# A 3x3 convolution with max pooling: input rows cast to bf16 by the loads, fewer five-product steps, and a new order of work

## The chip, the cores and the metric

The kernel runs on one core of a Trainium2 chip. The metric is device time in microseconds of that core, the median of several runs. A core has a matrix engine (PE, with its weight loads shown as PEld), a vector engine (DVE), a scalar engine (ACT), a general engine (POOL, also called GpSimd) and a queue engine (SP) that only issues DMAs here. Matrix products are summed in PSUM (8 banks of 128 x 512 f32); everything else lies in SBUF.

## The reference

The input x is 16 images of 64 channels, 64 by 64, in f32. The weights are 128 x 64 x 3 x 3. The reference pads each image by one, convolves, and takes the maximum of each 2 by 2 block:

```
x_pad = np.pad(x, ((0, 0), (0, 0), (pad, pad), (pad, pad)), mode='constant')
conv[b, co] += weight[co, ci, kh, kw] * x_pad[b, ci, kh:kh+h, kw:kw+w]
output[b, c, i, j] = np.max(conv[b, c, i*2:(i+1)*2, j*2:(j+1)*2])
```

The output is 16 x 128 x 32 x 32 in f32.

## The kernel before, in words

*Pairs, quarters, steps.* Two images (a pair p, 0 to 7) lie in one SBUF tile: image 0's 64 channels on partitions 0 to 63, image 1's on 64 to 127. Each image is cut into four quarters q of 16 rows, which give R = 8 rows of pooled output. A pair and a quarter are a step s, 32 in all. In a product the image number l (0 or 1, called a lane) picks one half of the PE array's rows, so that a matmul of lane 0 and one of lane 1 can run side by side. A matmul's output is 128 channels by 8 rows by 64 columns, one PSUM bank.

*Two convolution rows for one pooled row.* A step makes, per lane, a sum A and a sum B in two banks, from which the even and the odd convolution rows follow. Each product takes three matmuls, one per horizontal tap kw (`taps`, L406 to L421). There are two recipes, chosen per step by SEQ:

- A W step takes four products. Their inputs are made from the input rows first: E (differences of two neighbouring rows), S (sums) and V (differences of rows two apart; Ve and Vo are its two halves). P2 (on E) and P0 (on V) go to A. A is then copied to B (`seed`, L435, written SE in the order, SEv when DVE does it), P3 and P1 are added to B, and A's negative is evacuated (`evac`, EV, L429).
- A K step takes five products, PAa, PAb, PBa, PBb straight on bf16 input rows and PR on KS (a sum of neighbouring rows). It needs no seed and only the KS row operation.

After that both go on alike: the row maximum of B and the evacuated A (`rowmax`, MX, L449, DVE), a copy of the odd columns to SBUF (`odd`, OD, L472, ACT), and the maximum of even and odd columns (`colmax`, CM, L481, DVE), then the store (ST).

*Where the rows come from.* W steps read f32 tiles `wx` (four of them, each for a whole pair, with a row of zeros above and below); SP loads them (LX). K steps read bf16 tiles `kx` (a pool of 3); the first two K steps and step 2 go by way of an f32 tile `kf` and casts on ACT or DVE (XO, XE), the rest by a DMA from POOL's queue that casts on its way (LK, L275). Eight steps are K, 24 are W.

*Who makes the rows.* A suffix in the order names the engine: E.8:v on DVE, V.8:g on POOL, :a on ACT. For eleven W steps ACT first copies a row to a PSUM bank (`lift`, CP, L290), and DVE reads that copy beside the SBUF row (`two_rows`, L294). A row operation on POOL is made to wait for the last row operation that stands before it on DVE (`row_op`, L195 to L200).

*What sets the order.* ORDER is one list written out by hand, or rather by a search; each engine runs its part of it in order, and semaphores join the engines. Products are emitted in groups (`flush`): two products of different lanes give their taps by turns. `paced` (L251) makes a load wait until the step 12 (W) or 13 (K) before it has done its column maximum, since the tiles are used again.

*Head.* The weights are loaded first (LW), seven blocks of them are formed (c.D0, c.GS, ... on DVE; c.g0, c.g1, c.g2 on ACT), turned by PE (T) and copied out to SBUF (TV).

Of the kernel before, what the change touches and what calls it, by code (L numbers as in the profile page):

```python
# [9 lines left out]

SEQ = "KWKWWKWWWKWWWWKWWWKWWWWKWWWKWWWW"
ADDED = ()
ORDER = """
LW c.GS:v c.D2:v c.GM:v c.g1:a T.G1:0 T.D2:1 LX.1 c.D0:v c.g2:a E.1:v c.g0:a T.GM:2 TV.G1:a c.GP:v
T.G0:3 Ve.1:v T.D0:4 LX.0a TV.GM:a TV.G0:a TV.D0:a P2.1.1:5 P2.1.0:6 TV.D2:a SE.1.0:7 XO.0a:v T.G2:0
TV.G2:v SE.1.1:2 T.GP:3 Vo.1:v LX.0b PAa.0.1a:4 PAa.0.0a:1 XE.0a:a P0.1.0 P0.1.1 XO.0b:v S.1:v
PBa.0.0a:0 PAb.0.1a LX.3 P3.1.1 P3.1.0 TV.GP:a XE.0b:a LX.2 LX.4 PBa.0.0b PBa.0.1a:3 LX.6 EV.1.0  # L20
LK.5 PAb.0.0a PAa.0.1b EV.1.1 PBb.0.0a PBb.0.1a Vo.3:v KS.0:v MX.1.0 CP.3:6 PBa.0.1b PAa.0.0b Ve.3:g
PAb.0.1b PBb.0.0b PAb.0.0b PBb.0.1b XO.2:a XE.2:a E.4:g MX.1.1 EV.0.1 E.3:v P1.1.0 PAa.2.1:5 EV.0.0
PAa.2.0:4 P1.1.1 S.3:v MX.0.1 OD.1.0 OD.1.1 S.4:g Ve.4:g CP.6:6 PBa.2.0:1 PAb.2.1 MX.0.0 CM.1.0 LX.8
LX.7 CM.1.1 EV.2.1 PAb.2.0 PR.0.1 PR.0.0 PBa.2.1:7 EV.2.0 OD.0.0 OD.0.1 P2.3.0:2 P2.3.1:5 E.6:v
S.6:v KS.2:v CM.0.1 P2.4.0:4 PBb.2.1 CM.0.0 LX.10 LX.11 SE.3.1:6 PBb.2.0 P0.3.1 SE.4.0:3 SE.3.0:0
P0.4.0 P3.3.1 MX.2.1 EV.3.1 Vo.4:g EV.4.0 V.6:v P0.3.0 PR.2.1 LK.9 EV.3.0 LK.14 MX.2.0 MX.3.1
P2.4.1:5 P3.3.0 MX.3.0 P2.6.1:4 PR.2.0 SE.4.1:2 LX.12 OD.2.1 CM.2.1 OD.2.0 P1.3.1 P3.4.0 CM.2.0
S.7:g MX.4.0 OD.3.1 P1.3.0 P0.4.1 SE.6.1:7 OD.3.0 V.7:g EV.4.1 P2.6.0:1 P3.4.1 P0.6.1 P1.4.0 CM.3.1
SE.6.0:6 CM.3.0 E.7:v P3.6.1 PAa.5.0:5 EV.6.1 OD.4.0 V.10:g E.10:g MX.4.1 CM.4.0 MX.6.1 CP.8:4
PAa.5.1:0 P0.6.0 E.8:v P1.4.1 PAb.5.0 S.8:v EV.6.0 P3.6.0 PAb.5.1 EV.5.0 P2.7.1:3 PBa.5.0:1 EV.5.1  # L30
OD.4.1 MX.6.0 P1.6.1 P2.7.0:5 SE.7.1:0 PBa.5.1:4 PBb.5.0 OD.6.1 CM.4.1 S.10:v SE.7.0:2 P1.6.0 P0.7.1
KS.5:v CM.6.1 MX.5.0 P0.7.0 PBb.5.1 EV.7.1 EV.7.0 V.8:g P3.7.0 P2.10.1:7 PR.5.0 P3.7.1 MX.5.1 MX.7.0
PAa.9.0:3 PR.5.1 SE.10.1:5 OD.6.0 KS.14:v CM.6.0 V.11:g LX.16 P0.10.1 P1.7.0 MX.7.1 OD.5.0 OD.5.1
CM.5.1 OD.7.0 P3.10.1 P2.8.0:6 EV.10.1 SE.8.0:4 LX.15 LX.13 P1.7.1 PAb.9.0 EV.9.0 CM.5.0 MX.10.1
PBa.9.0:7 P2.8.1:1 OD.7.1 CM.7.0 KS.9:v P1.10.1 P0.8.0 SE.8.1:3 OD.10.1 CM.7.1 PAa.14.1:2 PBb.9.0
EV.8.0 LK.18 S.12:v E.12:g CP.11:0 CM.10.1 P3.8.0 P0.8.1 V.12:g PAa.9.1:6 P2.10.0:5 EV.8.1 MX.9.0
MX.8.0 SE.10.0:1 E.11:v PR.9.0 PAb.14.1 OD.9.0 PAb.9.1 P1.8.0 E.15:g EV.14.1 OD.8.0 P3.8.1 P0.10.0
S.11:v P2.11.1:0 PAa.14.0:2 CM.9.0 CP.13:7 CM.8.0 PBa.9.1:4 P3.10.0 MX.8.1 E.13:v EV.10.0 EV.9.1
P1.8.1 PAb.14.0 P2.11.0:5 PBb.9.1 MX.10.0 S.13:v SE.11.1:6 EV.14.0 OD.8.1 P1.10.0 P0.11.1 MX.9.1
SE.11.0:2 ST.5 OD.10.0 P3.11.1 P2.12.0:7 EV.11.1 CM.8.1 SE.12.0:3 ST.1 LX.17 ST.3 MX.11.1 ST.0  # L40
CM.10.0 P0.11.0 PR.9.1 OD.9.1 EV.11.0 V.13:g P2.13.1:0 P3.11.0 P0.12.0 P1.11.1 SE.13.1:1 CM.9.1
V.15:g MX.11.0 KS.18:v OD.11.1 CM.11.1 P3.12.0 P2.12.1:5 EV.12.0 SE.12.1:4 E.16:g P1.11.0 P0.13.1
LX.19 OD.11.0 MX.12.0 P3.13.1 PBa.14.0:7 EV.13.1 LX.20 P2.13.0:6 P0.12.1 LX.22 CM.11.0 PBb.14.0
# [40 lines left out]
def kernel(  # L84
# [7 lines left out]
    nc = tc.nc  # L92
# [13 lines left out]
    assert len(SEQ) == N  # L106

    const = ctx.enter_context(tc.tile_pool(name="const", bufs=1))
    kx_pool = ctx.enter_context(tc.tile_pool(name="kx_pool", bufs=3))
    row_pool = ctx.enter_context(tc.tile_pool(name="row_pool", bufs=8))  # L110
    v_pool = ctx.enter_context(tc.tile_pool(name="v_pool", bufs=6))
    vh_pool = ctx.enter_context(tc.tile_pool(name="vh_pool", bufs=4))
    ev_pool = ctx.enter_context(tc.tile_pool(name="ev_pool", bufs=8))
    od_pool = ctx.enter_context(tc.tile_pool(name="od_pool", bufs=6))
    od2_pool = ctx.enter_context(tc.tile_pool(name="od2_pool", bufs=4))
# [142 lines left out]
    def load(s, part, e):  # L258
# [11 lines left out]
        if e == "a":  # L270
            behind(inst, begun)
# [342 lines left out]
```

## Time and profile before

| what | value |
|---|---|
| median of 3 runs | 103.51 us (103.31 to 103.87) |
| span of the profiled execution, first to last instruction | 101.5 us |
| PE busy | 96.4 us, 870 matmuls |
| DVE busy | 91.4 us, 181 instructions |
| ACT busy | 89.5 us, 198 instructions |
| POOL busy | 79.3 us, 65 instructions |
| DMA | 24.07 MB, mean 237 GB/s |

The profiled execution has a span of 101.5 us; what lies around it is in the runs' times, whose median is 2.0 us more. Times in the profile count from the start of the span. In a row of a group stand the line, the engine, the operation, output and inputs, shape and count; then busy time in us, the mean of one in ns, and the idle time before it with what ended it. In a row of the timeline stand start and duration in us.

### The profile page before, as it was taken

What the parts mean: (1) busy time and instruction counts of PE and PEld (TensorE: products, weight loads), DVE (VectorE), ACT (ScalarE), POOL (GpSimd) and SP (SyncE); (2) the same over time, 40 slices, a digit from 0 to 9 for tenths busy, and PEclk for the clock granted to TensorE, in tenths of its full rate; (3) what the DMA queues carried; (4) which work ended last, traced back from release to release, by engine and by line L of the source; (5) the groups of instructions that cost most, each with busy time, mean ns of one, the idle gap of its engine ahead of it and who ended that gap; (6) DMA issues with size and microseconds to landing.
All of it is one profiled execution on the core that took longest, in us unless ns stands there. A gap on an engine that the chain in (4) does not pass through costs nothing.

```text
span 101.5 us, 2486 instructions
## 1 busy us (share of the span) xinstructions
PE 96.4 (95%) x870; PEld 55.6 (55%) x870; DVE 91.4 (90%) x181; ACT 89.5 (88%) x198; POOL 79.3 (78%) x65
## 2 busy tenths in 40 slices
PE   6999999999999999999989999999999999999950
PEld 2356885466666666555645555455475555655510
DVE  0599999999999999799999989998999999888980
ACT  5599999999988999998999989989989889899840
POOL 7000898988598599989999999998599999999000
PEclk9999999999999999999999999999999999999999
DMA  2999999991079989889998999999953915302353
GB/s 45 328 248 403 417 376 337 326 226 33 6 203 390 233 166 302 315 222 291 273 329 260 261 237 311 374 392 308 295 222 122 344 58 201 108 29 78 110 189 121
DMA packets 13789, 24.07 MB, mean 237 GB/s; under 512 B 1104, under 2 KB 9680, under 8 KB 13776
## 3 DMA queue, kind: packets, MB, share of 16 engines
q1 hardware_dynamic: 12624, 22.16, 64.9%
q0 software_dynamic: 864, 1.56, 10.2%
q10 hardware_dynamic: 288, 0.20, 0.6%
q8 instruction: 7, 0.11, 0.4%
q14 instruction: 6, 0.05, 0.1%
HBM read 17.07 MB, written 8.39 MB: 251 GB/s over the span
## 4 chain that ended last, share of the span: by engine, by line
PE 83%; ACT 6%; DVE 3%; DMA 3%; issue 2%; DVEq 0%; ACTq 0%
PE acc L414 80%; DMA wraw<-in_weight_dram 3%; ACT acc L445 3%; PE acc L229 2%; DVE acc L449 2%; ACT od L472 2%; ACT ev L429 1%; DVE o L481 1%; ACT wq L191 1%; DVE acc L443 0%; PE acc L439 0%; DVEq L609 0%; DVEq L449 0%; DVEq L443 0%; ACTq L290 0%
## 5 line engine op out<-in xcount | busy, mean ns | idle before, releaser
L414 PEld LDWEIGHTS <-wt 64*128 64x128 bf16 x840 | 52.8, 94 | 37.3 <-issue 2.5
L414 PE MATMUL acc<-wv,wt 64*128 64x504 bf16 (+1 forms) x228 | 49.5, 377 | 0.3 <-ACT acc L445 0.3
L449 DVE TENSOR_TENSOR acc<-acc,ev 128x512 f32<-128x512 f32 x64 | 42.9, 693 | 2.0 <-ACT ev L429 1.1
L196 POOL TENSOR_TENSOR wv<-wx 128x1024 bf16<-128x1024 f32 x18 | 42.3, 2362 | 2.5 <-DVE ks L196 1.6
L414 PE MATMUL acc<-kx,wt 64*128 64x504 bf16 (+6 forms) x216 | 38.9, 350 | 0.0
L414 PE MATMUL acc<-ws,wt 64*128 64x512 bf16 (+1 forms) x144 | 35.2, 377 | 0.2 <-DVE acc L449 0.2
L414 PE MATMUL acc<-we,wt 64*128 64x512 bf16 (+1 forms) x144 | 35.1, 377 | 0.0
L429 ACT ACTIVATE ev<-acc 128x512 f32<-128x512 f32 x48 | 28.6, 610 | 1.1 <-PE acc L414 1.0
L445 ACT COPY acc<-acc 128x512 f32<-128x512 f32 x45 | 26.3, 588 | 2.0 <-PE acc L414 0.4
L481 DVE TENSOR_TENSOR o<-acc,od 128x256 f32<-128x256 f32 (+1 forms) x65 | 25.7, 412 | 1.4 <-ACT od L472 0.5
L472 ACT COPY od<-acc 128x256 f32<-128x256 f32 x64 | 23.6, 382 | 2.7 <-PE acc L414 1.9
L196 POOL TENSOR_TENSOR we<-wx 128x512 bf16<-128x512 f32 x11 | 14.0, 1272 | 2.8 <-DVE ks L196 1.7
L414 PE MATMUL acc<-ks,wt 64*128 64x504 bf16 (+1 forms) x48 | 12.5, 377 | 0.0
L414 PE MATMUL acc<-vh,wt 64*128 64x504 bf16 (+1 forms) x60 | 10.4, 376 | 0.0
L196 POOL TENSOR_TENSOR ws<-wx 128x512 bf16<-128x512 f32 x8 | 10.1, 1268 | 0.1
L275 POOL DMA_DIRECT2D kx<-in_x_dram x6 | 3.5, 590 | 8.0 <-ACT ev L429 8.0
L431 ACT COPY ev<-acc 128x512 f32<-128x512 f32 x16 | 9.3, 598 | 0.4 <-PE acc L414 0.3
L196 POOL TENSOR_TENSOR vh<-wx 128x512 bf16<-128x512 f32 x7 | 8.8, 1272 | 0.5 <-DVE ks L196 0.4
L294 DVE TENSOR_TENSOR we<-acc,wx 128x512 bf16<-128x512 f32 x11 | 7.5, 682 | 0.0
L294 DVE TENSOR_TENSOR ws<-acc,wx 128x512 bf16<-128x512 f32 x11 | 7.5, 681 | 0.0
L290 ACT COPY acc<-wx 128x512 f32<-128x512 f32 x11 | 6.7, 607 | 0.1
L509 PE MATMUL acc<-const-bfloat16-1.0 128*128 128x512 bf16 x8 | 3.6, 625 | 0.8 <-PEq L595 0.8
(30 smaller groups left out, 34.3 us busy)
## 6 DMA issues: line engine op xcount, KB each, us to landing
out_dram<-o SPq DMA_DIRECT2D x30, 256.0 KB, 5.8
wx<-in_x_dram SPq DMA_DIRECT2D x12, 512.0 KB, 6.3
wx<-in_x_dram SPq DMA_DIRECT2D x6, 544.0 KB, 6.5
wx<-in_x_dram SPq DMA_DIRECT2D x6, 480.0 KB, 6.7
kx<-in_x_dram POOLq DMA_DIRECT2D x3, 256.0 KB, 7.2
kf<-in_x_dram SPq DMA_DIRECT2D x1, 512.0 KB, 7.7
kx<-in_x_dram POOLq DMA_DIRECT2D x2, 240.0 KB, 5.6
wraw<-in_weight_dram SPq DMA_DIRECT2D x1, 288.0 KB, 3.0
```

The lines of the kernel that those rows point to most:

```text
L196: inst = eng[e].tensor_tensor(out=out, in0=in0, in1=in1, op=op)
L275: paced(s, nc.gpsimd.dma_start(out=kx_of(p)[:, lo:hi, :], in_=rows_of(p, lo, hi)))
L290: nc.scalar.copy(out=acc[bank], in_=wrow(s, 0))
L294: nc.vector.tensor_tensor(out=t, in0=lifted[s], in1=wrow(s, 1), op=op)
L414: yield lambda kw=kw, o0=o0, o1=o1, c0=c0, c1=c1: nc.tensor.matmul(acc[t][:, i0:i1, o0:o1], wt[l * CI : l * CI + CI, K * BLOCKS[block] + T ...
L429: inst = nc.scalar.mul(t, acc[bank["A", s, l]], -1.0)
L431: inst = nc.scalar.copy(out=t, in_=acc[bank["A", s, l]])
L445: nc.scalar.copy(out=acc[b], in_=acc[bank["A", s, l]])
L449: nc.vector.tensor_tensor(out=t, in0=t, in1=ev[s, l], op=MAX)
L472: nc.scalar.copy(out=od[s, l][:, i0:i1], in_=acc[bank["B", s, l]][:, i0:i1, 1::2])
L481: done[s, l] = nc.vector.tensor_tensor(out=outs(s)[:, l, i0:i1], in0=acc[bank["B", s, l]][:, i0:i1, 0::2], in1=od[s, l][:, i0:i1], op=MAX,)
L509: nc.tensor.matmul(acc[n], ones[:, 0:128], ones, start=True, stop=True, skip_group_check=True)
```

## The change

- Seven of the eight pairs (all but pair 1) lie in bf16 in one tile `narrow_x`, padded by a row of zeros above and below, each pair with a place of its own for the whole kernel. Nine casting DMAs from POOL's queue fill it (LH, `load_cast`): five of half a pair, four of a whole pair. Steps 0 and 2 (quarters 0 and 1 of pair 0) still come as f32 in `kf` and are cast by ACT and DVE. Pair 1 stays f32 in `wide_x`, loaded by SP. `paced` is gone: no load waits for a tile.
- SEQ has four K steps (0, 2, 12, 22) and 28 W steps. A K step reads `narrow_x` itself.
- `lift` is gone with the eleven copies to PSUM. Row operations read two SBUF rows, bf16 but for pair 1. POOL makes 18 E, 17 S, 7 V and 4 halves of V; DVE makes the rest, among them 16 V.
- The evacuated A, the odd columns and the output of a step lie in tiles for both lanes; some steps do both lanes in one instruction (a 2 in the order: EV.0.2, MX.1.2, OD.1.2, CM.1.2).
- ORDER is new. A token of a product now gives one tap, not three, so that taps of any two products can alternate. All seven weight blocks are formed and turned before the first product. Seeds on ACT are 53 where they were 45; seeds on DVE stay three.

```diff
-SEQ = "KWKWWKWWWKWWWWKWWWKWWWWKWWWKWWWW"
+SEQ = """
+K00 W10 K01 W11 W12 W13 W02 W03 W20 W21 W22 W23 K30 W31 W32 W33 W40 W41 W42 W43 W50 W51 K52 W53 W60 W61 W62
+W63 W70 W71 W72 W73
+"""
+WIDE = (1,)
+CASTS = ((0, 2, 4), (2, 0, 2), (2, 2, 4), (3, 0, 2), (3, 2, 4), (4, 0, 4), (5, 0, 4), (6, 0, 4), (7, 0, 4))
...
+    wide_x = const.tile([128, len(WIDE), H + 2, W], FP32, name="wide_x")
+    narrow_x = const.tile([128, len(narrow), H + 2, W], BF16, name="narrow_x")
...
-    def paced(s, inst):
...
+    def load_cast(k):
+        p, q0, q1 = CASTS[k]
+        lo, hi = chunk(q0, q1)
+        inst = nc.gpsimd.dma_start(out=xs[p][:, lo + 1 : hi + 1, :], in_=rows_of(p, lo, hi))
+        if k == 0:
+            behind(inst, named["begun"])
...
-    def lift(s, bank):
-
-        lifted[s] = acc[bank]
-        nc.scalar.copy(out=acc[bank], in_=wrow(s, 0))
...
+    def two_rows(s, name, e):
+        pool, a, b, op = {
+            "KS": (ks_pool, 0, 1, ADD),
+            "S": (row_pool, 0, 1, ADD),
+            "E": (row_pool, 0, 1, SUB),
+            "Ve": (vh_pool, 1, -1, SUB),
+            "Vo": (vh_pool, 2, 0, SUB),
+        }[name]
+        tag = {"KS": "ks", "S": "ws", "E": "we", "Ve": "vh", "Vo": "vh"}[name]
+        t = row[name, s] = pool.tile([128, R, W], BF16, name=tag)
+        row_op(e, t, rows_at(s, a), rows_at(s, b), op)
...
         if name in PRODUCTS:
...
+            if what not in going:
+                s, l = int(args[0]), int(args[1][0])
+                if at:
+                    bank[PRODUCTS[name][0], s, l] = int(at)
+                going[what] = taps(name, s, l, args[1][1:])
+            next(going[what])()
```

The new order begins and, around step 21 and at its end, runs like this:

```
LW LX.1 LX.0a LX.0b LX.3 LX.2 LX.4 LX.5 c.D0:v c.g0:a c.GS:v c.g1:a T.D0:0 c.D2:v T.G0:1 c.g2:a T.G1:2
c.GM:v TV.G0:a T.G2:3 c.GP:v TV.G1:a T.GM:4 TV.D0:a T.D2:1 E.1:v TV.GM:a T.GP:2 TV.D2:a S.1:v P2.1.1:4
P2.1.0:0 TV.G2:a P2.1.1 P2.1.0 P2.1.1 P2.1.0 XE.0a:v XO.0a:a Ve.1:v PBa.0.1a:3 SE.1.1:5 PBa.0.1a PAa.0.0a:7
...
P0.15.1 P2.14.0 P0.15.1 OD.13.0 P1.10.0 P0.15.1 E.21:v P1.10.0 SE.14.0:2 P3.15.1 P1.10.0 CM.13.0 P3.15.1
...
MX.31.1 P1.30.1 P3.31.0 P1.29.0 OD.30.1 P1.29.0 P1.31.1 MX.31.0 P1.29.0 P1.31.1 P1.30.0 P1.31.1 OD.29.0
P1.30.0 CM.30.1 P1.30.0 OD.31.1 P1.31.0 CM.29.0 ST.30.1 OD.30.0 P1.31.0 CM.31.1 ST.29.0 P1.31.0 CM.30.0
ST.31.1 OD.31.0 ST.30.0:a CM.31.0a ST.31.0a CM.31.0b ST.31.0b:a
```

More of the change, by code (lines that the diff above doesn't have):

```diff
@@ L21 @@
[L21 to L31, printed above, removed]
@@ L127, in behind, with chunk @@
             tc.add_manual_dep(inst.ins, other.ins.name, SYNC, reason="order")
-    kinds = {k: [s for s in range(N) if SEQ[s] == k] for k in "KW"}
-    nk = len(kinds["K"])
-    place = {s: divmod(i, NQ) for i, s in enumerate(kinds["K"] + kinds["W"])}
-    assert all(SEQ[s] == "K" for s in kinds["K"][:2])
+    kind = [t[0] for t in steps]
+    place = [(int(t[1]), int(t[2])) for t in steps]
+    assert sorted(place) == [divmod(i, NQ) for i in range(N)]
     def rows_of(p, lo, hi):
         return x[2 * p : 2 * p + 2].rearrange("b c h w -> (b c) h w")[:, lo:hi, :]
-    def chunk(s):
-        p, q = place[s]
-        same = any(place[t] == (p, q - 1) and SEQ[t] == SEQ[s] for t in range(N))
-        lo = 2 * R * q + 1 if same else max(0, 2 * R * q - 1)
-        return p, lo, min(H, 2 * R * (q + 1) + 1)
+    def chunk(q0, q1):
+        return max(0, 2 * R * q0 + min(q0, 1)), min(H, 2 * R * q1 + 1)
     def half(s):
         return 2 * R * place[s][1] + R + 1
-    NWX = 4
-    wx = [const.tile([128, H + 2, W], FP32, name=f"wx_{i}") for i in range(NWX)]
-    for t in wx:
-        nc.gpsimd.memset(t[:, 0, :], 0.0)
-        nc.gpsimd.memset(t[:, H + 1, :], 0.0)
-    kx = {}
-    def kx_of(p):
-        if p not in kx:
-            kx[p] = kx_pool.tile([128, H, W], BF16, name="kx")
-        return kx[p]
+    narrow = [p for p in range(B // 2) if p not in WIDE]
+    wide_x = const.tile([128, len(WIDE), H + 2, W], FP32, name="wide_x")
+    nc.gpsimd.memset(wide_x[:, :, 0 : H + 2 : H + 1, :], 0.0)
+    xs = {p: wide_x[:, i] for i, p in enumerate(WIDE)}
     BLOCKS = {m: i for i, m in enumerate(("D2", "G0", "D0", "G2", "GM", "G1", "GP"))}
@@ L170 @@
     zeros = const.tile([128, 512], BF16)
-    begun = nc.gpsimd.memset(zeros, 0.0)
+    nc.gpsimd.memset(zeros, 0.0)
+    narrow_x = const.tile([128, len(narrow), H + 2, W], BF16, name="narrow_x")
+    nc.gpsimd.memset(narrow_x[:, :, 0 : H + 2 : H + 1, :], 0.0)
+    xs.update({p: narrow_x[:, i] for i, p in enumerate(narrow)})
     wv = wraw.rearrange("a (c k) -> a k c", k=K * K)
@@ L190, in cast @@
         if e == "a":
-            nc.scalar.copy(out=out, in_=in_)
-        else:
-            last_row[0] = eng[e].tensor_copy(out=out, in_=in_)
+            return nc.scalar.copy(out=out, in_=in_)
+        last_row[0] = eng[e].tensor_copy(out=out, in_=in_)
+        return last_row[0]
     def row_op(e, out, in0, in1, op):
@@ L247, with load @@
     kf = {}
-    done = {}
-    AHEAD = {"W": 12, "K": 13}
-    def paced(s, inst):
-        for l in (0, 1):
-            behind(inst, done.get((s - AHEAD[SEQ[s]], l)))
-        if SEQ[s] == "K" and s < AHEAD["K"] and s not in kf:
-            behind(inst, done["head"])
-    def load(s, part, e):
-        p, lo, hi = chunk(s)
-        if SEQ[s] == "W":
-            t = wx[p % NWX]
-            paced(s, nc.sync.dma_start(out=t[:, lo + 1 : hi + 1, :], in_=rows_of(p, lo, hi)))
+    named = {}
+    def load(s, part):
+        p, q = place[s]
+        lo, hi = chunk(q, q + 1)
+        if p in WIDE:
+            nc.sync.dma_start(out=xs[p][:, lo + 1 : hi + 1, :], in_=rows_of(p, lo, hi))
             return
@@ L284, with rows_at @@
     row = {}
[L285 to L298 removed]
+    def rows_at(s, a):
         p, q = place[s]
         f = 2 * R * q + a + 1
[L302 removed]
@@ L324, in rs_cast @@
-    def rs_cast(s, e):
-        t = row["S", s] = row_pool.tile([128, R, W], BF16, name="ws")
-        cast(e, t, wrow(s, 0))
-    def re(s, e):
-        t = row["E", s] = row_pool.tile([128, R, W], BF16, name="we")
-        two_rows(s, t, e, SUB)
-    def re_half(s, part, e):
-        if part == "a":
-            row["E", s] = row_pool.tile([128, R, W], BF16, name="we")
-        i0, i1 = PARTS[part]
-        row_op(e, row["E", s][:, i0:i1], wrow(s, 0)[:, i0:i1], wrow(s, 1)[:, i0:i1], SUB)
-    def rv(s, e):
+        return xs[p][:, f : f + 2 * R - 1 : 2, :]
@@ L341, in rv @@
         f = 2 * R * q
-        u = wx[p % NWX]
-        row_op(e, t, u[:, f + 2 : f + 2 + 2 * R, :], u[:, f : f + 2 * R, :], SUB)
-    def rv_half(s, e, odd):
-        p, q = place[s]
-        t = row["V" + "eo"[odd], s] = vh_pool.tile([128, R, W], BF16, name="vh")
-        f = 2 * R * q + odd
-        u = wx[p % NWX]
-        row_op(e, t, u[:, f + 2 : f + 1 + 2 * R : 2, :], u[:, f : f + 2 * R - 1 : 2, :], SUB)
+        row_op(e, t, xs[p][:, f + 2 : f + 2 + 2 * R, :], xs[p][:, f : f + 2 * R, :], SUB)
     bank = {}
@@ L424, with of_step, sums, columns @@
     ev, od, ot = {}, {}, {}
+    def of_step(table, pool, name, shape, s):
+        if s not in table:
+            table[s] = pool.tile([128, 2] + shape, FP32, name=name)
+        return table[s]
+    def sums(side, s, l):
+        a = acc[bank[side, s, 0 if l == 2 else l]]
+        if l < 2:
+            return a
+        gap = (bank[side, s, 1] - bank[side, s, 0]) * R * W
+        return bass.AP(tensor=a.tensor, offset=a.offset, ap=[a.ap[0], [gap, 2], *a.ap[1:]])
+    def columns(a, parity):
+        return a[..., parity::2]
+    def lanes(t, l):
+        return t if l == 2 else t[:, l]
     def evac(s, l):
-        t = ev[s, l] = ev_pool.tile([128, R, W], FP32, name="ev")
-        if SEQ[s] == "W":
-            inst = nc.scalar.mul(t, acc[bank["A", s, l]], -1.0)
-        else:
-            inst = nc.scalar.copy(out=t, in_=acc[bank["A", s, l]])
-        if (s, l) == (1, 0):
-            done["head"] = inst
+        t = lanes(of_step(ev, ev_pool, "ev", [R, W], s), l)
+        if kind[s] == "W":
+            nc.scalar.mul(t, sums("A", s, l), -1.0)
+        else:
+            nc.scalar.copy(out=t, in_=sums("A", s, l))
     def seed(s, l, e):
@@ L511 @@
         )
-    unit = []
-    def flush():
-        for group in zip(*unit):
-            for tap in group:
-                tap()
-        unit.clear()
-    lane = [None]
+    going = {}
     for token in ORDER.split():
@@ L525 @@
         if name in PRODUCTS:
[L526 to L539 removed]
+            if what not in going:
[4 more added lines that the diff above has]
+            next(going[what])()
+        elif name == "c":
             weights(args[0], at)
@@ L572 @@
                 seed(s, l, name[2:])
-                continue
-            if name in ("OD", "CM", "RM"):
-                {"OD": odd, "CM": colmax, "RM": pairmax}[name](s, l, part)
-            else:
-                {"EV": evac, "MX": rowmax}[name](s, l)
-    flush()
+            elif name == "EV":
+                evac(s, l)
+            elif name == "MX":
+                rowmax(s, l)
+            elif name == "ST":
+                store(s, l, part, at)
+            elif name == "OD":
+                odd(s, l)
+            else:
+                colmax(s, l, part)
+    assert all(next(t, None) is None for t in going.values())
 _INS = ['x', 'weight', 'pool_size']
```

294 lines of the change are left out of this document (122 added, 172 removed).

## The prediction

> **What bounds the kernel now.** I read the head of the page first, then busy time by stretch, the chain that ended last, and the order of instructions on DVE and POOL.
>
> ```profile
> span 101.5 us, 2486 instructions
> ...
> PE 96.4 (95%) x870; PEld 55.6 (55%) x870; DVE 91.4 (90%) x181; ACT 89.5 (88%) x198; POOL 79.3 (78%) x65
> ```
>
> Four engines are at 78% or more, so what helps one only pays if the others follow. The stretches:
>
> ```profile
> 8.00:88.00 80.00, 79.70 (x757) 47.33 (x758) 77.46 (x153) 74.89 (x168) 71.71 (x46) 1.00 0.83 259
> 88.00:98.60 10.60, 9.63 (x82) 5.12 (x78) 9.52 (x20) 9.14 (x22) 5.79 (x5) 1.00 0.34 112
> ```
>
> After the span of time come PE, weight load, DVE, ACT and POOL, then the granted clock (1.00: no throttling) and the DMA. For 80 us PE is full, with DVE 2.5 us and ACT 5 us behind it. The chain says the same:
>
> ```profile
> 8.04 44.13 PE acc L414 x418
> ...
> 53.10 34.67 PE acc L414 x316
> ...
> 96.44 1.41 PE acc L414 x6
> ...
> 98.28 0.29 DVE o L481
> ```
>
> 78.8 us of the chain are matmuls, and 44.13 / 418 is 0.106 us for each. So PE bounds up to 88 us; from there ACT and DVE pieces alternate, and the span ends 2.9 us after the last maximum's 98.6.
>
> A second bound shows in no share. DVE and POOL in order of time:
>
> ```profile
> 26.68 0.41 DVE L481 TENSOR_TENSOR o<-acc,od 128x256 f32<-128x256 f32 x1
> 27.02 0.68 DVE L196 TENSOR_TENSOR ws<-wx 128x512 bf16<-128x512 f32 x1
> 27.61 0.42 DVE L196 TENSOR_TENSOR ks<-kx 128x512 bf16<-128x512 bf16 x1
> 27.95 0.42 DVE L481 TENSOR_TENSOR o<-acc,od 128x256 f32<-128x256 f32 x1
> ...
> 30.14 0.62 DVE L196 TENSOR_TENSOR ks<-kx 128x512 bf16<-128x512 bf16 x1
> ```
>
> ```profile
> 11.13 1.28 POOL L196 TENSOR_TENSOR vh<-wx 128x512 bf16<-128x512 f32 x1
> ...
> 28.11 2.37 POOL L196 TENSOR_TENSOR wv<-wx 128x1024 bf16<-128x1024 f32 x1 [1.23 <-DVE ks L196]
> 30.84 2.37 POOL L196 TENSOR_TENSOR wv<-wx 128x1024 bf16<-128x1024 f32 x1 [0.36 <-DVE ks L196]
> ...
> 86.38 3.73 POOL L196 TENSOR_TENSOR vh<-wx 128x512 bf16<-128x512 f32 x3
> ...
> 92.52 1.27 POOL L196 TENSOR_TENSOR ws<-wx 128x512 bf16<-128x512 f32 x1
> ```
>
> Start to start, DVE pays 0.59 us for an f32 operation of 512 columns and 0.34 for a column maximum or a bf16 KS. The KS at 27.61 ran with POOL idle in 0.42; the one at 30.14 met a POOL operation running until 30.48, took 0.62, and ended 0.28 after POOL. POOL starts again 0.08 after the KS (30.76 to 30.84). So a DVE operation with both inputs in SBUF and a POOL operation take turns; call that the shared port. The Trainium skill says so outright ("SBUF — State Buffer", Who interferes with whom: such a DVE instruction contends with a POOL one that reads SBUF, and the loser blocks fully); the KS row agrees.
>
> **The change, part by part.**
>
> ```profile
> L196 POOL TENSOR_TENSOR wv<-wx 128x1024 bf16<-128x1024 f32 x18 | 42.3, 2362 | 2.5 <-DVE ks L196 1.6 <-DVE we L196 0.7 <-DVE ws L196 0.2
> ...
> L445 ACT COPY acc<-acc 128x512 f32<-128x512 f32 x45 | 26.3, 588 | 2.0 <-PE acc L414 0.4 <-DVE o L481 0.3 <-ACT od L472 0.3
> ...
> L290 ACT COPY acc<-wx 128x512 f32<-128x512 f32 x11 | 6.7, 607 | 0.1
> ...
> L196 DVE TENSOR_TENSOR wv<-wx 128x1024 bf16<-128x1024 f32 x1 | 1.3, 1315 | 0.0
> ...
> L171 POOL MEMSET zeros<- 128x512 bf16 x1 | 0.5, 525 | 0.0
> ```
>
> *PE.* Four steps lose a product: four times six taps, 840 to 816. Twelve taps of K steps' edge rows (64 columns fewer) become whole. 24 x 0.106 less 12 x 0.013: -2.4 us. Against it: the two images of a pair use one half of the array each (tile 64*128 in the row at 6.51 below), and 0.106 is half of a pair's time. A tap with no neighbour of the other image takes a pair's time alone, 0.106 more. Down the old order 4 taps stand alone, all in the last group; down the new one about 22: 12 before the last fifty (three PR.2.1 in a row, three P0.5.1, halves of step 0), ten in the end. 18 x 0.106 is +1.9 if all of them cost, 0 if PE would have waited there for the other image. I take half, +0.9.
>
> *ACT.* 11 lifts go: two evacuations in 1.10 us overlap by some 0.06 each, so 11 x 0.55 = -6.0. Four more W steps want eight seeds, of which all go to ACT (45 to 53): 8 x 0.53 = +4.2. One turn-out moves over from DVE (+0.4), four steps copy odd columns of both images at once (-0.4). Sum -1.8, for an engine with some 5 us to spare in 80.
>
> *DVE.* Rows before: 22 lifted at 0.59, ten f32 at 0.59, eight KS, one V at 1.23: 23.2 us. Rows after: 7 f32 at 0.59, one V at 1.23, 24 bf16 of 512 at 0.34, 15 bf16 V. A bf16 V is not in the trace: at least 0.34, at most the f32 1.23; twice the columns of KS without its fixed part gives 0.61, which I take. 22.7 us. Double-width maxima of four steps save 0.5, the turn-out 0.3: sum -1.3.
>
> *POOL and the port.* POOL goes from 26 operations of 512 and 18 of 1024 to 39 and 7. At today's 1.235 start to start (three in 3.73) and 2.33 that is 74.1 to 64.5 us. DVE's two-SBUF rows rise from 10.2 to 22.7, for the lifted ones read PSUM and took no turn. Port: 84.3 to 87.2 us, and some 15 more hand-overs at 0.08. What POOL needs for bf16 inputs no row shows: from below its memset of the same columns, 0.53; from above the f32 row, 1.27. Ten bytes an element become six while the count stays; I take 1.15 from start to start, close to the f32 row, and 1.9 times that for 1024, which takes (34 + 6 x 1.9) x 0.085 = 3.9 us off the port (five of the 39 and one of the seven still read f32). At that price it is no bound.
>
> *Head.* All seven weight blocks are turned before the first product, and P2's block (GM) is fourth among ACT's turn-outs, where it was second.
>
> ```profile
> 6.31 1.24 ACT L240 COPY wt<-acc 128x384 bf16<-128x384 bf16 x3
> ...
> 6.51 0.87 PE L414 MATMUL acc<-we,wt 64*128 64x512 bf16 x6
> ```
>
> ACT's turn-outs begin near 5.6 (after three casts) at 0.43 each, so the fourth ends near 7.4: P2.1 starts 0.9 late. XO.0a on ACT comes two turn-outs later, near 8.6, so dense work starts at 8.65 instead of 8.04, with three half taps already done: +0.45.
>
> *Loads and queues.* SP keeps 7 input loads and its stores; nothing on it waits for a buffer any more. POOL issues nine casting loads for six; the first waits for ACT's last cast of step 0 (near 9.9), and behind it on POOL queue two more loads and S.4, whose first reader, P1.4.1, comes some 85 taps later: hidden. POOL's first row operation moves from 11.13 to about 12.7, since it follows S.3 on DVE.
>
> *Idle of PE.* From 8.04 to 97.85 PE spent some 3 us beyond its taps: 1 us near 52 behind ACT's lift, 2 in the end. The lift's place is gone: -0.5.
>
> Sum: -2.4 + 0.9 + 0.45 - 0.5 = -1.5 us on PE's path. ACT (-1.8) and DVE (-1.3) follow almost as far, so I keep it: 101.5 - 1.5 = 100.0 us of span. The median of the runs, 103.51, stands 2.0 over the span; with the same margin 102.0.
>
> **The rivals.**
>
> *The port decides (slower).* If bf16 rows cost POOL what f32 rows do, its turns end late. From 12.7: 64.5 of POOL, 17.5 of DVE's rows not yet done, 22 hand-overs 1.8, and 1 us of idle as now: 97.5 instead of 93.8 for the last ws. Behind it stand P1.31, the last copy and maxima, as now from 96.44 to 98.58: 2.1. End 99.6, +1.0: 104.5, and up to 106.5 if DVE's maxima are held up behind blocked rows. It decides from about 1.2 us an operation on. For it: an operation's 1024 columns cost 2.36 and 512 cost 1.27, 2.1 ns a column, so columns set the time; against it, nothing on POOL here has 16-bit inputs. The Trainium skill takes this side ("GPSIMD Engine Reference", 2.1 Instruction dispatch: two inputs share one read port, about 2.5 cycles an element whatever DVE does); at its 1.2 GHz that is an estimate of 2.1 ns, and the f32 rows agree. By that rule the time is 104.5.
>
> *A casting load is late.*
>
> ```profile
> q1 hardware_dynamic: 12624, 22.16, 64.9%
> q0 software_dynamic: 864, 1.56, 10.2%
> ```
>
> The seventh cast (pair 5, whole) must land before E.21, a DVE row 367 whole taps down the order: 8.65 + 360 x 0.107 and the lone taps make 48 us. Up to it 4.6 MB of bf16 are cast: at q0's rate (10.4 us for 1.56 MB) 30.6 us, and 13 stores 3.4 MB at q1's 10.1. From 10.5 plus a first latency of 1.5 that is 52.7, some 4 us late, on DVE, which is only 1 to 2 us from being the bound: 3 us reach the end, 105. Against it, q0's share holds time beside other transfers; at q1's rate for the source bytes the casts take 27.5 us, and 1.5 us remain, which my case gives to DVE's distance.
>
> *More is won.* If all lone taps stand where PE waited anyhow, and half of the end's 2 us goes with ACT's lighter load: -1.5 - 0.9 - 1.0, so 100.1.
>
> **How the numbers follow.** My case 0.54 (own range 100.8 to 103.3), the port 0.24, the late load 0.11, more won 0.11. About 0.5% is what a measurement here can tell: 103.0 and 104.0. My case gives 0.46 faster and 0.08 same; more won 0.11 faster; port and load 0.30 slower, 0.03 same, 0.02 faster. Faster 0.59, same 0.11, slower 0.30. The range leaves out the far end of either side: 100.1 to 104.9.
>
> **What would show it.** Right: POOL's 512 rows from narrow_x at or under 1.2 us, V on DVE near 0.7 with few longer, PE full from 8.7 us to near 88, and no gap of 1 us in the middle. Wrong: DVE rows stretched to 1 us and more behind POOL, POOL's last row after 95 us, a DVE wait on a narrow_x load near 48 us, PE waiting on row tiles.

## The result, and the profile after

The changed kernel takes 106.38 us (median of 4 runs, 106.32 to 106.73) where the kernel before takes 103.41 (median of 4 runs beside it). The ratio is 1.026, with a 95% interval of 1.020 to 1.032: slower by 2.6%. The forecast was 102.0, and its range ended at 104.9. The profiled execution has a span of 104.5 us, 3.0 more than before.

The head of the page and the busy time by stretch, cut where the prediction cut them:

```profile
span 104.5 us, 2395 instructions
...
PE 95.2 (91%) x845; PEld 59.5 (57%) x845; DVE 91.2 (87%) x179; ACT 88.0 (84%) x191; POOL 66.5 (64%) x64
```

```profile
8.00:88.00 80.00, 76.92 (x713) 49.92 (x712) 74.82 (x147) 71.77 (x157) 55.91 (x48) 1.00 0.78 190
88.00:101.00 13.00, 11.99 (x100) 7.05 (x96) 12.15 (x25) 10.71 (x25) 8.52 (x8) 1.00 0.33 111
```

PE, DVE, ACT and POOL are all less busy than before, and yet from 8 to 88 us PE did 713 matmuls where it had done 757. It stood idle for 3.1 us of those 80. The chain that ended last says where:

```profile
9.19 0.30 DVE narrow_x L215
...
9.54 1.15 PE acc L379 x14
...
10.77 1.02 ACT ev L414
...
11.83 6.99 PE acc L379 x65
...
18.85 1.24 DVE acc L430
...
20.13 7.11 PE acc L379 x62
...
27.26 0.63 ACT acc L426
...
27.94 72.06 PE acc L379 x640
```

The matmuls run unbroken from 27.94 us to 100.00. Before that point the chain leaves PE four times, and PE's own rows there carry what they waited for in brackets (the last row, of its own, is ACT's):

```profile
9.54 0.92 PE L379 MATMUL acc<-narrow_x,wt 64*128 64x256 bf16 x13 [0.65 <-DVE narrow_x L215]
...
11.83 0.59 PE L379 MATMUL acc<-vh,wt 64*128 64x504 bf16 x3 [1.05 <-ACT ev L414]
...
20.13 0.37 PE L379 MATMUL acc<-narrow_x,wt 64*128 64x504 bf16 x1 [1.32 <-DVE acc L430]
```

```profile
20.11 0.59 ACT L414 COPY ev<-acc 128x512 f32<-128x512 f32 x1 [1.68 <-DVE acc L430]
```

The second and the third of PE's rows are odd. At 11.83 P0.1.1, which adds to bank 4, waits for ACT's EV.0.2, which reads banks 7 and 1. At 20.13 PAb.2.0, which adds to bank 1, waits for DVE's maximum MX.3.2 on banks 0 and 7. Neither uses a bank or a tile of the instruction that it waits for. Nor does ACT's EV.2.1, which reads bank 4 and waits 1.68 us for the same maximum. Both releasers are instructions on both images, whose two banks are six and seven apart.

The count of taps shows how the span grew. PE's taps before and after 28 us, first of the kernel before, then of the changed one (a tap that runs at 28.00 is counted in both rows):

```profile
0.00:28.00 28.00, 20.90 (x212) 1.00 0.79 249
28.00:101.00 73.00, 69.33 (x632) 1.00 0.76 234
```

```profile
0.00:28.00 28.00, 17.85 (x175) 1.00 0.94 242
28.00:101.00 73.00, 71.99 (x642) 1.00 0.63 159
```

By 28 us the changed kernel is 37 taps behind. It has 24 fewer in all, but ten or so more left, and takes 72.0 us for 642 of them (0.1121 each) where before 632 took 69.85, up to 97.85 (0.1105 each). Ten taps are 1.1 us, and the lower rate is about as much; so PE ends 2.15 later. The rate is lower between 28 and 44 us only: 143 taps where the kernel before has 152, and from 44 to 92 us 441 matmuls in both. The last 0.85 comes behind the last maximum: 2.73 us from the end of its record to the end of the span before (98.77 to 101.5), 3.58 after (100.92 to 104.5). The very last store among the DMA issues, size and time to landing, before and then after (the one ahead of it took the same):

```profile
out_dram<-o ACTq DMA_DIRECT2D x1, 64.0 KB, 1.7
```

```profile
out_dram<-o ACTq DMA_DIRECT2D x1, 64.0 KB, 2.4
```

### The profile page after: what moved, and what is told of

Its sections match the earlier page's. It is cut to its first block, busy times and chain, and to the rows that moved or that the text cites. A ratio compares the mean times of both kernels' runs of the same rounds, so it can differ in the third digit from the quotient of the medians.

```text
span 104.5 us, 2395 instructions
## 1 busy us (share of the span) xinstructions
PE 95.2 (91%) x845; PEld 59.5 (57%) x845; DVE 91.2 (87%) x179; ACT 88.0 (84%) x191; POOL 66.5 (64%) x64
## 4 chain that ended last, share of the span: by engine, by line
PE 84%; DMA 7%; ACT 2%; DVE 2%; SPq 1%; issue 1%; DVEq 0%; ACTq 0%
PE acc L379 84%; DMA kf<-in_x_dram 7%; DVE acc L430 1%; ACT ev L414 1%; ACT acc L426 1%; SPq L282 0%; SPq L277 0%; SPq L475 0%; ACT od L434 0%; DVE narrow_x L215 0%; DVE o L444 0%; DVEq L537 0%; ACTq L414 0%
## 5 line engine op out<-in xcount | busy, mean ns | idle before, releaser
L379 PE MATMUL acc<-wv,wt 64*128 64x504 bf16 (+1 forms) x276 | 55.7, 376 | 0.1
L430 DVE TENSOR_TENSOR acc<-acc,ev 128x512 f32<-128x512 f32 (+1 forms) x61 | 42.3, 718 | 2.4 <-PE acc L379 1.0
L444 DVE TENSOR_TENSOR o<-acc,od 128x256 f32<-128x256 f32 (+2 forms) x61 | 25.0, 431 | 2.5 <-ACT od L434 1.7
L434 ACT COPY od<-acc 128x256 f32<-128x256 f32 (+1 forms) x60 | 22.7, 395 | 2.4 <-PE acc L379 2.1
L219 POOL TENSOR_TENSOR we<-narrow_x 128x512 bf16<-128x512 bf16 x16 | 18.3, 1149 | 9.9 <-DVE ws L219 4.1
L379 PE MATMUL acc<-narrow_x,wt 64*128 64x504 bf16 (+6 forms) x120 | 19.3, 331 | 2.0 <-DVE acc L430 1.3
L219 POOL TENSOR_TENSOR ws<-narrow_x 128x512 bf16<-128x512 bf16 x15 | 17.2, 1152 | 5.8 <-PE acc L379 1.9
L219 POOL TENSOR_TENSOR wv<-narrow_x 128x1024 bf16<-128x1024 bf16 x6 | 12.7, 2126 | 1.0 <-DVE ws L219 1.0
L219 DVE TENSOR_TENSOR wv<-narrow_x 128x1024 bf16<-128x1024 bf16 x15 | 10.7, 720 | 0.0
L379 PE MATMUL acc<-ks,wt 64*128 64x504 bf16 (+1 forms) x24 | 5.4, 376 | 0.0
```

The costliest lines, as they stand in the source:

```text
L219: inst = eng[e].tensor_tensor(out=out, in0=in0, in1=in1, op=op)
L379: yield lambda kw=kw, o0=o0, o1=o1, c0=c0, c1=c1: nc.tensor.matmul(acc[t][:, i0:i1, o0:o1], wt[l * CI : l * CI + CI, K * BLOCKS[block] + T ...
L430: nc.vector.tensor_tensor(out=t, in0=t, in1=lanes(ev[s], l), op=MAX)
L434: nc.scalar.copy(out=lanes(t, l), in_=columns(sums("B", s, l), 1))
L444: nc.vector.tensor_tensor(out=t, in0=columns(a, 0), in1=u, op=MAX)
```

## The experiments

Theory A was that an instruction on two far banks holds up the work on every bank between them. Its rivals were that ACT and DVE are late in the head in any case (B), that the taps without a neighbour cost the time (C), and that the second half of step 0's load does (D). All kernels below are edits of the changed one. "Split" is the kernel of the second experiment, which most later ones start from. The kernel before, run beside each group, stood at 103.46 to 103.52.

**Other bank numbers.** Each bank gets a new number: 0 to 0, 1 to 2, 2 to 3, 3 to 4, 4 to 5, 5 to 7, 6 to 6, 7 to 1. EV.0.2 then reads banks 1 and 2, MX.3.2 works on 0 and 1. The instructions and their order are the same.

```diff
-... PAa.0.0a:7 ... PAa.0.1a:1 ... SE.3.1:7 ... SE.3.0:0 ... SE.10.1:5 ... SE.10.0:4 ... SE.14.1:6
+... PAa.0.0a:1 ... PAa.0.1a:2 ... SE.3.1:1 ... SE.3.0:0 ... SE.10.1:7 ... SE.10.0:5 ... SE.14.1:6
```

> The changed kernel with its PSUM banks renumbered, one new number for each old one, so that the two lanes of the copy EV.0.2 and of the maximum MX.3.2 lie in neighbouring banks (0 and 1) and not six or seven apart. No instruction is added, dropped or moved. Theory A (an instruction on two far banks holds up the work on every bank between them): the two PE idles of 1.05 us near 11.8 and 1.32 us near 20.1 go, and the time falls from 106.4 by 1.9 to 2.4, to 104.0 to 104.5. Rival B (these waits are real lateness of ACT and DVE in the head, which any order of banks has): no change within 0.5, 105.9 to 106.9. Rival C (the taps that stand alone set the loss): no change either.

Measured: 104.38 us (10 runs), 2.0 less. Both odd waits are gone. What PE waited for (us in all, times, longest), and then PE in order of time near 52 us:

```profile
PE acc L379 <- DVE o L444: 0.8, 1, 0.8
...
PE acc L379 <- DVE narrow_x L215: 0.5, 1, 0.5
PE acc L379 <- ACT wt L263: 0.3, 1, 0.3
```

```profile
52.35 0.39 PE L379 MATMUL acc<-wv,wt 64*128 64x504 bf16 x2 [0.82 <-DVE o L444]
```

A wait of 0.82 us is new, and it is of the same kind. The renumbering pulled apart the banks of step 10, which had been neighbours: CM.10.2 now works on 5 and 7, and P3.14.1, next in line, adds to bank 6 between them. So theory A is shown twice, by the waits that went and by the one that came. Whether the wait is made by the program's semaphores or by the chip itself, no run here tells.

**Both far instructions split.** The banks stay as they were.

```diff
-P0.1.0 EV.0.2 P0.1.1 ... P2.4.1:5 MX.3.2 PAb.2.0
+P0.1.0 EV.0.1 EV.0.0 P0.1.1 ... P2.4.1:5 MX.3.1 MX.3.0 PAb.2.0
```

> The same two instructions written one lane at a time (EV.0.1, EV.0.0 and MX.3.1, MX.3.0), banks as they were. Theory A: the same gain less the fixed part of two more instructions, 104.1 to 104.7. Rival B: 105.9 to 106.9. If this gains clearly more than the renumbering, the halves' earlier ends matter and not the span between the banks.

Measured: 103.39 us (10 runs; ratio to the kernel before 0.998, interval 0.994 to 1.002). That is 3.0 us less than the changed kernel: the whole of what the change had lost. The chain now reaches its unbroken stretch 2.74 us earlier, and the stretch is as long as in the changed kernel:

```profile
25.20 72.08 PE acc L379 x640
```

The forecast, 104.1 to 104.7, was too high, and it had named a sign: a gain clearly beyond the renumbering's would speak for the earlier ends of the halves. The chain of the renumbered kernel says otherwise. It leaves the head at the same time, breaks at step 10, and PE ends there 0.83 later (98.11 beside 97.28):

```profile
25.21 23.97 PE acc L379 x214
...
52.35 45.76 PE acc L379 x409
```

**Only the maximum split.**

```diff
-P2.4.1:5 MX.3.2 PAb.2.0
+P2.4.1:5 MX.3.1 MX.3.0 PAb.2.0
```

> Only MX.3.2 is written one lane at a time. Theory A: the 1.32 us idle near 20.1 goes and the 1.05 us one near 11.8 stays, 105.0 to 105.4. Rival B: 105.9 to 106.9.

Measured: 104.65 us, 1.7 less than the changed kernel; the wait behind EV.0.2 is there still (1.01 us). So the maximum cost 1.7, more than the 1.0 to 1.4 forecast, and the copy 1.3.

**The head in another order,** on the renumbered banks.

```diff
-XO.0b:v ... XE.0b:a ... Vo.1:v ... SE.1.0:6 ... PAa.0.0b ... PAb.0.1b ... P0.1.0 P0.1.1 ... EV.0.2 ... P3.1.1 ... EV.1.1
+SE.1.0:6 ... Vo.1:v XO.0b:v ... XE.0b:a ... P0.1.0 P0.1.1 ... P3.1.0 P3.1.1 ... PAa.0.0b ... PAb.0.1b ... EV.1.1 EV.1.0 ... EV.0.2
```

> The renumbered banks, and in the head P0.1 and P3.1 are moved ahead of the products of step 0 that need the second half of its load; SE.1.0 goes ahead of ACT's cast of that half and Vo.1 ahead of DVE's. Theory D (the load's second half, 0.65 us of PE idle near 9.5, is the other part of the head's loss): 0.5 to 0.9 below the renumbered kernel, 103.2 to 103.9. If the head is bound by ACT and DVE instead, the same as the renumbered one within 0.3.

Measured: 105.04 us, 0.7 more than the renumbered kernel: a miss. PE in order of time no longer waits for the load, but for E.1 ahead of P2.1 and for EV.0.2, which now stands behind EV.1 on ACT. E.1 had waited 0.63 us for its own load, which the edit does not touch, and the profiled execution is the slowest of the four; so not all of the 0.7 is the order's:

```profile
7.56 0.83 PE L379 MATMUL acc<-we,wt 64*128 64x512 bf16 x6 [0.98 <-DVE we L219]
12.82 0.83 PE L379 MATMUL acc<-we,wt 64*128 64x512 bf16 x6 [0.44 <-ACT ev L414]
```

**Loads held back.** Split, with the loads of steps 2, 4 and 5 waiting for DVE's cast of step 0's first half.

```diff
-LX.3 LX.2 LX.4 LX.5 ... XE.0a:v XO.0a:a
+LX.3 ... XE.0a:v LX.2 LX.4 LX.5 XO.0a:a
+        behind(inst, named.get("begun"))
```

> The kernel with the two far-bank instructions split (103.39), in which the loads of steps 2, 4 and 5 are held back until DVE has cast the first half of step 0, so that the second half of step 0 shares the DMA engines with less. Theory D (that half lands at 9.1 and PE idles 0.69 us for it): it lands near 8.5, the idle goes or falls to 0.2, and the time is 102.7 to 103.0. If ACT's and DVE's chain of the head sets the pace behind it, 103.2 to 103.6 with the idle gone. If the held-back loads come late for S.4 or for the cast of step 2, above 103.6 with a wait on wide_x or kf between 12 and 20 us.

Measured: 105.18 us. The idle near 9.5 is gone, and the third case came true: S.4 waits for its load, E.4 behind it on POOL is late for PE, and a casting load is late for V.6 on DVE (issued at 9.14 us, it lets V.6 start at 18.86). POOL and PE in order of time:

```profile
14.38 1.68 POOL L219 TENSOR_TENSOR ws<-wide_x 128x512 bf16<-128x512 f32 x1 [3.49 <-DMA wide_x<-in_x_dram]
```

```profile
17.34 0.37 PE L380 MATMUL acc<-we,wt 64*128 64x512 bf16 x1 [0.86 <-POOL we L219]
```

The DMA engines are full up to 28 us in the split kernel (the shares of 1.04 in its rows further down), and here what one early load gained another lost.

**Taps without a neighbour left out.** Split, without PR.2.1 and P0.5.1.

```diff
-PR.2.1 PR.2.1 ... PR.2.1 ... P0.5.1 ... P0.5.1 ... P0.5.1
```

> The split kernel without two products of three taps, PR.2.1 and P0.5.1 (so steps 2 and 5 miss them in their output): these six taps stand alone, with no tap of the other image beside them. If a lone tap costs a pair's time (0.213 us), 6 x 0.213 = 1.3 us less: 102.1. If PE would have waited there anyway, 103.2 to 103.5. Half of it, as the prediction took: 102.7.

Measured: 103.96 us; nothing is gained. All six taps had filled waits. Where PR.2.1 was, PE now waits 0.45 us for a row maximum; where P0.5.1 was, it waits 0.62 us for ACT's seed SE.7.0, which P0.7.0 needs. PE in order of time, then the chain:

```profile
22.36 0.37 PE L379 MATMUL acc<-ks,wt 64*128 64x512 bf16 x1 [0.45 <-DVE acc L430]
...
25.75 0.37 PE L379 MATMUL acc<-wv,wt 64*128 64x512 bf16 x1 [0.62 <-ACT acc L426]
```

```profile
25.75 71.57 PE acc L379 x637
```

The stretch is 0.5 shorter than the split kernel's only because P0.5.1 no longer opens it. It ends at 97.32, there at 97.28. So the price of these six taps is 0 and not 0.213 each. Why the median lies 0.5 above the split kernel's is not shown; the profiled execution took 103.65.

**Paired taps left out.** Split, without P0.18 of both images, near 60 us.

```diff
-P0.18.0 P0.18.1 ... P0.18.0 P0.18.1 P0.18.0 ... P0.18.1
```

> The split kernel without P0.18 of both images (step 18 misses it in its output): six taps in the steady part that stand in pairs with each other. If PE is the bound there, 6 x 0.107 = 0.64 us less: 102.75. If DVE and ACT set the pace there and PE only looks full, 103.2 to 103.5; then the 24 taps that the change takes away are worth less than the 2.4 us of the prediction.

Measured: 103.93 us; again nothing is gained. The chain shows a new break where the taps went, a wait for a V and a maximum on DVE:

```profile
9.70 0.31 DVE narrow_x L215
...
25.73 36.95 PE acc L379 x327
...
62.72 0.29 DVE wv L219
63.01 0.62 DVE acc L430
...
63.68 34.11 PE acc L379 x300
```

From 25.73 to 97.79 it is 72.06, as with the taps. That it starts 0.5 later than in the split kernel is no work of the taps: DVE's cast of the second half of step 0, the first row shown, starts 0.6 later (9.11 there), since the load came later in this execution.

**No double instruction at all.** The split kernel with MX.1, MX.0 and OD and CM of steps 1, 0, 5 and 10 one image at a time (`MX.1.2` becomes `MX.1.1 MX.1.0`, and so on).

> Every remaining instruction on both images (MX.1, MX.0, OD and CM of steps 1, 0, 5, 10) is written one image at a time; their banks were neighbours or two apart. If only the far spans cost, the ten more instructions cost ACT and DVE 0.3 and 0.4 us of fixed parts, and the time is 103.3 to 103.8. If near spans and the later ends of double instructions cost too, 102.7 to 103.1.

Measured: 103.39 us, the same. The stretch is 0.3 shorter (71.77) and starts 0.1 later. Double instructions on near banks cost 0.3 us at most, and they win nothing either.

**V rows left out.** Split, without six V rows of DVE (steps 18, 19, 21, 23, 24, 25).

```diff
+            if name == "V" and s in RAW:
+                return pk(block, at, first)(s, l, part)
...
+        if s in RAW:
+            return
```

> The split kernel (103.39) without the V rows of steps 18, 19, 21, 23, 24 and 25, all of them DVE's; P0 and P3 of these steps read the bf16 input rows in their place (so these steps are not computed as they should be). DVE has 6 x 0.6 = 3.6 us less to do between some 50 and 72 us, PE has the same taps. If DVE alone sets the pace of the steady part: 1.5 to 3.6 less, 99.8 to 101.9. If PE does (77 taps in 8 us are its peak): 103.1 to 103.5.

Measured: 103.56 us (ratio to the kernel before 1.000, interval 0.998 to 1.002). DVE's 3.6 us alone are worth next to nothing; the stretch is 0.2 shorter (71.87).

**Both left out.** The same, and P0.18 gone as well.

> The same, and P0.18 of both images is left out as well (six paired taps, 0.64 us of PE). Taking them away alone gave nothing (103.93 beside 103.39). If PE and DVE bind together there, so that neither alone pays, both together pay PE's 0.64 below the one before: 102.5 to 102.9. If neither binds (ACT, or the waits between the engines), the same as the one before.

Measured: 103.06 us (9 runs; ratio to the kernel before 0.995, interval 0.992 to 0.998), 0.5 less than without the V rows alone. The stretch, in two pieces around one maximum:

```profile
25.15 36.84 PE acc L385 x327
...
62.07 0.71 DVE acc L436
...
62.82 33.92 PE acc L385 x300
```

It ends at 96.74, 71.59 after its start. In five kernels that do the same work in the same order from there on (the changed one, split, only the maximum split, loads held back, and the filled head below) the stretch is 72.05 to 72.09 long. Leaving out the taps shortens it by nothing, the V rows by 0.2, both by 0.48: more than the two alone, less than PE's 0.64. So PE and DVE hold each other there, at least in part. The medians alone would not carry this, for the intervals of the last two kernels just touch.

**The idle of the head filled.** Split, with SE.1.0 and Vo.1 ahead of the casts that wait, and P0.1 ahead of step 0's second half.

```diff
-XO.0b:v ... XE.0b:a ... Vo.1:v ... PAa.0.0b SE.1.0:6 ... P0.1.0 P0.1.1
+SE.1.0:6 Vo.1:v XO.0b:v ... XE.0b:a ... P0.1.0 P0.1.1 ... PAa.0.0b
```

> The split kernel with three moves in the head and nothing left out: ACT's SE.1.0 and DVE's Vo.1 go ahead of their casts of the second half of step 0 (both engines stand idle there, 0.64 and 0.79 us), and the six taps of P0.1 go ahead of the products that need that half. If these idles are part of the loss in the head, PE's 0.69 us near 9.5 is filled and the time is 102.6 to 103.0; if a later bound of the head (ACT's copies near 24 us) sets the pace, 103.2 to 103.5.

Measured: 103.83 us (10 runs; ratio to the kernel before 1.003, interval 1.000 to 1.007), no gain. PE's idle is filled, but the last stretch begins at 25.07, only 0.1 ahead of the split kernel's. DVE, now free earlier, waits for step 3's load instead, as its order in time shows:

```profile
10.20 0.69 DVE L219 TENSOR_TENSOR we<-wide_x 128x512 bf16<-128x512 f32 x1 [0.36 <-DMA wide_x<-in_x_dram]
```

**Step 2's casts on POOL.** The kernel without double instructions, with XO.2 and XE.2 moved.

```diff
-XO.2:a ... XE.2:a
+LH.2 XO.2:g XE.2:g
+        if e == "g":
+            return nc.gpsimd.tensor_copy(out=out, in_=in_)
```

> The kernel with every instruction one image at a time (103.39), in which the two casts of step 2's rows (XO.2 and XE.2, 0.62 us each, 128x512 f32 to bf16) go from ACT to POOL, ahead of S.4, where POOL stood idle 1.5 us. Nothing is left out. Theory E (ACT's chain of copies and casts sets the pace of the head until 25.3 us, where the last unbroken stretch of matmuls begins): that stretch begins 0.6 to 1.1 earlier and the time is 102.3 to 102.9, below both kernels. If DVE or the row tiles set the pace there as well, 103.2 to 103.5 with the same start of the stretch. If POOL's rows for step 4 come late behind the casts (E.4 is first read near 18.3), above 103.6 with PE waiting on a row tile near 18.

Measured: 103.89 us (9 runs; ratio 1.004, interval 1.002 to 1.006), a miss. ACT is free, and waits. The casts take 1.0 us each on POOL, and DVE's S.3 beside them 1.09, where the same row took 0.68 in the split kernel; PE then waits 0.37 for the maximum behind it. POOL and DVE in order of time:

```profile
11.96 2.01 POOL L216 CAST narrow_x<-kf 128x512 bf16<-128x512 f32 x2
```

```profile
12.40 1.09 DVE L221 TENSOR_TENSOR ws<-wide_x 128x512 bf16<-128x512 f32 x1
```

No version here that does all of its work beats the kernel before by more than the intervals allow.

## Why the prediction was wrong, point by point

*The step that failed: the head, +0.45.* The prediction priced the later P2.1 and the casts, and stopped there. P2.1 came out better than priced (at 7.07, 0.56 late and not 0.9); what it left out is the size of the miss. The 37 taps that are missing at 28 us are 4.1 us at 0.111 each. The split kernel has 198 taps in its row up to 28 us, so 23 of the 37 (2.6 us) are the two waits behind the far-bank instructions; with what follows from them they are the 3.0 us that splitting wins. The prediction met the instructions on both images twice, as -0.4 on ACT and -0.5 on DVE, and looked at what they save, not at what waits for them. It had no rival for it, though the bank numbers that tell of it (`PAa.0.0a:7`, `PAa.0.1a:1`) stand in the order itself. And what they should have saved came to nothing: without any of them the time is the same.

*The rest of the head.* Fourteen taps, 1.5 us, are behind in the split kernel as well. Busy time by stretch in the kernel before, then in the split one, then DVE in order of time in the split kernel and in the kernel before:

```profile
6.00:12.00 6.00, 6.00 (x79) 4.38 (x79) 6.00 (x13) 6.00 (x14) 1.57 (x2) 1.00 1.01 381
12.00:20.00 8.00, 8.00 (x76) 4.89 (x72) 8.00 (x15) 7.49 (x17) 7.45 (x8) 1.00 1.04 352
20.00:28.00 8.00, 8.00 (x77) 5.25 (x75) 7.87 (x18) 7.46 (x18) 6.18 (x4) 1.00 0.44 97
```

```profile
6.00:12.00 6.00, 4.99 (x63) 3.49 (x61) 5.10 (x10) 5.31 (x14) 1.76 (x3) 1.00 1.04 366
12.00:20.00 8.00, 8.00 (x83) 4.43 (x80) 8.00 (x12) 7.08 (x14) 5.95 (x6) 1.00 1.04 218
20.00:28.00 8.00, 7.87 (x69) 4.06 (x67) 8.00 (x20) 7.54 (x18) 5.32 (x4) 1.00 1.04 234
```

```profile
9.11 0.29 DVE L215 CAST narrow_x<-kf 128x256 bf16<-128x256 f32 x1 [0.83 <-DMA kf<-in_x_dram]
...
10.41 0.69 DVE L219 TENSOR_TENSOR we<-wide_x 128x512 bf16<-128x512 f32 x1
...
12.76 2.35 DVE L430 TENSOR_TENSOR acc<-acc,ev 128x1024 f32<-128x1024 f32 x2
```

```profile
10.48 1.29 DVE L449 TENSOR_TENSOR acc<-acc,ev 128x512 f32<-128x512 f32 x2
```

From 12 to 28 us DVE is as good as full in both kernels. What differs is the stretch ahead: there DVE was busy for all of the 6 us and now is for 5.10. It waits 0.83 us for the second half of step 0's load, and its first maximum starts at 12.76 where it started at 10.48 before, for E.3, V.3 and S.3, all on the f32 pair, now stand ahead of it too. So theory D has its part. Five profiled executions have the same order up to 25 us, but for the two split instructions, and no far-bank wait in it (the renumbered kernel, split, P0.18 left out, the V rows left out, both left out). In them DVE's cast of that half starts between 9.10 and 9.70 us, and the last stretch 16.0 to 16.2 us later each time. Yet filling PE's idle, unloading ACT and giving that load more room each left the start of the last stretch within 0.13 or made it later, as DVE then waited for another load or met POOL's work. That the load sets when DVE's row of work begins, and that row how long the head takes, is argued from these rows; no run here took work from DVE in the head. POOL's later start was in the prediction (12.7 us, measured 13.13) without a price.

*PE, -2.4.* The count was right, 24 taps fewer. Their worth was not: near 60 us six more taps are worth 0 alone, DVE's rows 0.2 alone, and both together 0.5. The prediction said that ACT and DVE "follow almost as far" and so kept the sum. ACT's busy time fell by 1.5 us (1.8 forecast), but DVE's by 0.2 (91.4 to 91.2; 1.3 forecast). Where DVE follows by less than PE's gain, it takes the gain back.

*Lone taps, +0.9, and the idle near 52, -0.5.* The idle is gone, as said. Together these two should have made 0.4; the lower rate from 28 us on makes about 1. The six lone taps that were left out were all free, so the other case of the prediction, that PE would have waited there, held for them, and not its half. The other lone taps were not tried. What lowers the rate between 28 and 44 us is not settled.

*The end, 0.* The stores behind the last maximum cost 0.85 more, which no step had. The last two stores land in 2.4 us and not 1.7, beside four others sent within 2 us; that these others are the cause was not tried.

*The port.* Right to leave it out. POOL's bf16 rows, against the threshold of 1.2 us from start to start:

```profile
L219 POOL TENSOR_TENSOR we<-narrow_x 128x512 bf16<-128x512 bf16 x16 | 18.3, 1149 | 9.9 <-DVE ws L219 4.1 <-DVE we L219 2.4 <-DVE wv L219 1.1
L219 POOL TENSOR_TENSOR wv<-narrow_x 128x1024 bf16<-128x1024 bf16 x6 | 12.7, 2126 | 1.0 <-DVE ws L219 1.0
L219 DVE TENSOR_TENSOR wv<-narrow_x 128x1024 bf16<-128x1024 bf16 x15 | 10.7, 720 | 0.0
```

POOL stood idle before its rows and waited for DVE's, so it did not set the pace, though its last row ended after 95 us: that sign, which the prediction had named against itself, only told that everything was late (in the split kernel it ends at 94.2). The Trainium skill ("GPSIMD Engine Reference", 2.1 Instruction dispatch) gives about 2.5 cycles an element as the floor for two inputs; at the 1.2 GHz that the page gives this is an estimate of 2.1 ns a column, and the section makes no difference by type. The trace does not quite agree: 512 more columns of bf16 cost 977 ns, 1.9 ns each. DVE's V took 0.60 from start to start in the middle of the run, 0.61 forecast.

*The late casting load.* Not seen in the changed kernel: no row operation waits for a load of `narrow_x`. The first latency of 1.5 us in that rival's sum stands in no row; the loads of `narrow_x` landed in 6.6 to 14.1 us, 8.9 in the median. Held-back loads brought it about at another place (V.6, 18.8 us).

## What to carry to other kernels

An instruction on two buffers of one tile can hold up everything that lies between them; before two such operations are joined, lay the buffers side by side, or look in the trace for a matmul that waits on an instruction whose banks it does not touch. A renumbering of the buffers, with no instruction changed, tells such a wait from a real one. When two engines are both nearly full, work taken from one can be worth nothing until the other is relieved at the same place, so a gain is to be priced on both. And work that fills a wait costs nothing: before it is priced, look what its engine would have waited for.

## What the runs showed of the hardware that was not expected

- bf16 inputs make a POOL row only 10% quicker than f32 ones (1149 ns against 1.27 us for 512 columns, 2126 against 2362 for 1024), though an element is six bytes in all and not ten. On DVE the V row goes from 1218 ns to 720.
- A PE that is 8.00 of 8.00 us busy can lose taps without the time falling (six near 60 us): the row of a tap is 0.38 us long while taps start 0.11 apart, so the busy time hides small waits.
- A cast from f32 to bf16 of 512 columns took 1.0 us on POOL, beside rows of DVE, and 0.62 on ACT.
- One transfer of 256 KB, the second half of step 0, landed up to 0.6 us later from one execution to the next, and the start of the last stretch moved with it (25.15 to 25.73 us).
